# First MLP's input: seven block forms built behind one transposition of each token block

## The chip, the cores and the metric

The kernel runs on one core of one Trainium2 chip. The metric is device time in microseconds (us) of one execution. The core's engines run beside one another, each through a queue of its own: TensorE (PE in the profile; its weight loads are PEld), VectorE (DVE), ScalarE (ACT), GpSimd (POOL), and SyncE (SP), which here issues most of the transfers.

## The reference

A trunk of two layers over 1024 tokens of width 1024, all in float32. Layer 0 mixes tokens with a gated linear recurrence (HGRN2), layer 1 with a causal convolution module; a squared-ReLU MLP follows each mixer, with a layer norm after each part:

```python
for i in range(2):
    mix = hgrn2_mixer(x, ...) if i == 0 else conformer_conv_mixer(x, ...)
    x = layer_norm(ALPHA * x + mix, ln_mix_g[i], ln_mix_b[i])
    ff = jnp.square(jax.nn.relu(x @ ffn_w1[i])) @ ffn_w2[i]      # 1024 -> 4096 -> 1024
    x = layer_norm(ALPHA * x + ff, ln_ffn_g[i], ln_ffn_b[i])
```

The change is in layer 0, between the layer norm behind the mixer and `x @ ffn_w1[0]`.

## The kernel before, in words

**Split numbers.** A float32 operand is held as two parts, hi (a ScalarE copy that rounds) and lo (a VectorE subtraction of hi from the number), and a product is three TensorE passes, hi·hi, hi·lo and lo·hi. Making the two parts is called a split here (`split`, line 1042; for weights `Slots.split`, line 71).

**Block forms.** The first matrix product of the MLP is done as seven block products in place of eight. The input is four blocks: y[n] is the half n of the tokens (512 of them, as four token blocks t of 128), and k is the half of the 1024 columns; below, "nk" is the block of token half n and column half k. The seven products need the input in seven forms, all with the columns on the partitions, so transposed: form 1 is 00, form 2 is 01, form 5 is 00 − 10, form 6 is −(form 5) − 11, form 7 is 11 − 10, form 3 is 11, and form 4 is −(form 6) − 01. The weights come in seven forms as well, sums of four loaded blocks (`Forms.unit`, line 130). The product order is 1, 2, 6, 5, 7, 3, 4 for each of eight column groups c of the MLP; only at the start it is (c0, 1), (c0, 2), (c1, 1), (c1, 2), and then the others of c0 and of c1. One product of `Up.form` (line 1186 on) is twice 12 matmuls of 512 columns.

**Where the forms come from.** After the output projection of the mixer, `norm` (line 1091) finishes a token block y[n][:, t]. Before the change, forms 5, 6, 4 and 7 are made in token layout, by VectorE, 128x512 at a time (`forms_of`, line 1119, into the buffers `ts`, `t4s` and `t7s`), and each is then transposed by itself: `turn` (line 1096) does four 128x128 transpositions on TensorE into one of two PSUM banks (`aux`), and a split from that bank writes the form's slice for this t. In all there are seven such turns for each t, 28, so 112 transpositions.

**The order.** `bg.chores` is a list of closures, and each `product` takes one off the list behind its matmuls. From the end of the mixer on this is only the order of the program text: the framework's scheduler then lays the instructions of each engine, and of SP's queue, by text order among those whose inputs its own model holds ready. So the order in the trace can differ from that of the text. Waits follow whole buffers: a new view over the place of an old one waits until every access to the old one is done.

**Buffers that matter here** (in KB of each partition): `ts` at 200 and 202; the raw weight blocks of `Forms` at 192, 196, 200 and 204, so that the third lies over both `ts`; its sums at 160 and 162 on; its slots at 144, 152, 48, 112 and 120, where 144 holds the weights of (c1, 2) before and 48 is also the place of `t7s`; the layer norm's gain and offset at 192 and 196.

In the profile nearly all TensorE and VectorE work has line 204, the wrapper that counts costs. L1045 is the hi copy of a split, L72 that of the weights, L135 the load of a raw weight block, L1105 `keep` (the copy of y to HBM for the later residual), L1224 the first copy out of a product's bank.

Of the kernel before, what the change touches and what calls it, by code (L numbers as in the profile page):

```python
# [8 lines left out]
F32 = mybir.dt.float32  # L9
# [3 lines left out]
ALU = mybir.AluOpType  # L13
PSUM = bass.MemoryType.PSUM

P = 128
D = 1024
# [3 lines left out]
HT = 512  # L21
NTB = HT // P
# [141 lines left out]
class LateForms(Forms):  # L164

    turned = True
# [102 lines left out]
def body(ctx, tc, d, out):  # L269
    nc = tc.nc  # L270
# [9 lines left out]
    def view(kb, shape, dt=F32, name="t"):  # L280
        at, top = int(kb * 1024), KBYTES * 1024
        if at < edge[0]:
            if edge[0] < top:
                space.tile([P, (top - edge[0]) // 4], F32, name="gap")
            edge[0] = 0
        if at > edge[0]:
            space.tile([P, (at - edge[0]) // 4], F32, name="gap")
        edge[0] = at + (prod(shape) + 7) // 8 * 32
        return space.tile([P, *shape], dt, name=name)

    def ring(kbs, shape, name, dt=F32):
        return Ring([view(kb, shape, dt, name) for kb in kbs])

    def run(kb, n, size):
        return [kb + i * size for i in range(n)]

    def slots(kbs, name):
        return ring(kbs, (2, 1024), name, F32R)

    def raws(kbs, name="raw"):  # L300
        return ring(kbs, (1024,), name)
# [21 lines left out]
    bg = Background()  # L323
    vector = Clocked(nc.vector, bg.dve, vector_cost)
    tensor = Clocked(nc.tensor, bg.pe, tensor_cost)
# [6 lines left out]
    def aux():  # L332
        return rings["aux"]().rearrange("p (a b) -> p a b", a=NTB)
# [40 lines left out]
    ident = cst.tile([P, P], F32, name="ident")  # L374
    wide_t, rows = (HT,), (NTB, P)

    XF, VS, VO = {}, {}, {}
    x00, x10, x01, x11, t6 = [view(kb, (4, HT), F32, "xr") for kb in run(112, 5, 8)]
# [663 lines left out]
    def split(hi, lo, ps, scale=None):  # L1042

        if scale is None:
            nc.scalar.copy(out=hi, in_=ps)  # L1045
            vector.tensor_tensor(out=lo, in0=ps, in1=hi.bitcast(F32), op=ALU.subtract)
        else:
            nc.scalar.activation(hi, ps, AF.Copy, scale=scale)
            vector.scalar_tensor_tensor(out=lo, in0=ps, scalar=scale, in1=hi.bitcast(F32), op0=ALU.mult, op1=ALU.subtract)
# [7 lines left out]
    def gain(kb, name, layer):  # L1057
        return vec(kb, f"{name}_g", layer), vec(kb + 4, f"{name}_b", layer)
# [12 lines left out]
    def moments(yt):  # L1071
        bs = stat.tile([P, 2, 6], F32, tag="bs", name="bs")
        for j in range(2):
            half_stats(bs, yt, j)
        mv = rstd_of(bs)
        return mv[:, 0:1], mv[:, 3:4]
# [14 lines left out]
    def norm(yt, g, b):  # L1091
        mu, rs = moments(yt)
        vector.scalar_tensor_tensor(out=yt, in0=yt, scalar=mu, in1=g, op0=ALU.subtract, op1=ALU.mult)
        vector.scalar_tensor_tensor(out=yt, in0=yt, scalar=rs, in1=b, op0=ALU.mult, op1=ALU.add)

    def turn(yt, xt, t, k0, nk):

        for k in range(0, nk, 4):
            pt = aux()
            for j in range(4):  # L1100
                tensor.transpose(pt[:, j, :], yt[:, (k0 + k + j) * P : (k0 + k + j + 1) * P], ident)
            split(xt[:, 0, k : k + 4, t * P : (t + 1) * P], xt[:, 1, k : k + 4, t * P : (t + 1) * P], pt)

    def keep(half, t, src):
        nc.sync.dma_start(out=kept[half][t], in_=src)  # L1105
# [10 lines left out]
    def blocks(name, layer, c):  # L1116
        return [d[name][layer, c, q] for q in range(4)]

    def forms_of(x, out, only=(5, 6, 7, 4)):

        t = {i: out(i) for i in only}
        if 5 in only:
            vector.tensor_tensor(out=t[5], in0=x[0][0], in1=x[0][1], op=ALU.subtract)
            vector.scalar_tensor_tensor(out=t[6], in0=t[5], scalar=-1.0, in1=x[1][1], op0=ALU.mult, op1=ALU.subtract)
        if 7 in only:
            vector.tensor_tensor(out=t[7], in0=x[1][1], in1=x[0][1], op=ALU.subtract)
        if 4 in only:
            vector.scalar_tensor_tensor(out=t[4], in0=t[6], scalar=-1.0, in1=x[1][0], op0=ALU.mult, op1=ALU.subtract)
        return t
# [3 lines left out]


    g, b = gain(192, "ln_mix", 0)
    y = [view(160 + 16 * h, (NTB, D), F32, "y") for h in range(2)]
    for half in range(2):
        for t in range(NTB):
            nc.sync.dma_start(out=y[half][:, t], in_=d["x"][half * HT + t * P : half * HT + (t + 1) * P])
    ts, t4s = ring(run(200, 2, 2), wide_t, "t"), ring(run(212, 4, 2), wide_t, "t4")  # L1140
    early = [Slots(nc, vector, slots((204,), "fw"), raws((0,))), Slots(nc, vector, slots((112, 120), "fw"), raws((96, 100)))]
    early.append(Slots(nc, vector, slots((144,), "fw"), raws((152,))))

    xf = {i: view(kb, (2, 4, HT), F32R, f"x1f{i}") for i, kb in ((6, 0), (5, 16), (3, 32), (1, 64), (2, 80), (7, 96), (4, 128))}
    early[0].plan(blocks("w1q", 0, 0)[:1])
    early[1].plan([blocks("w1q", 0, 0)[1], blocks("w1q", 0, 1)[0]])
    early[2].plan(blocks("w1q", 0, 1)[1:2])
    yb = [[[y[n][:, t, k * HT : (k + 1) * HT] for n in range(2)] for k in range(2)] for t in range(NTB)]
    tt = {}

    def x1_form(t, i, src=None, k=0):
        turn(tt[t][i] if src is None else src, xf[i], t, k, 4)

    def x1_block(half, t):
        norm(y[half][:, t, :], g, b)
        if half == 0:
            bg.chores += [lambda: x1_form(t, 1, y[0][:, t, :]), lambda: x1_form(t, 2, y[0][:, t, :], 4)]
            return
        tt[t] = forms_of(yb[t], lambda i: (t4s if i == 4 else ts)(), (5, 6, 4))
        keep(0, t, y[0][:, t, :])  # L1160
        if t < NTB - 1:
            bg.chores += [lambda: x1_form(t, 6), lambda: x1_form(t, 5)]

    for half in range(2):
        for t, n in early_out + ((0, 1), (1, 1), (3, 0), (2, 1), (3, 1)) if half == 0 else [(t, n) for t in range(NTB) for n in range(2)]:
            ps = acc()
            if half or (t, n) not in early_out:
                product(ps, wide(oT[half], t, ws[n]))
            yv = y[half][:, t, n * HT : (n + 1) * HT]
            vector.scalar_tensor_tensor(out=yv, in0=yv, scalar=ALPHA, in1=ps, op0=ALU.mult, op1=ALU.add)  # L1170
            if n == 1:
                if half == 1 and t == 0:
                    early[0].ahead(1)
                x1_block(half, t)
                if half == 0 and t:
                    bg.chore()
# [232 lines left out]
            nc.sync.dma_start(out=raw, in_=d[name][at])  # L1409
            staged.append((name, at))  # L1410

    t7s = ring((48, 50), wide_t, "t7")
    fw = Forms(nc, vector, slots((144, 152, 48, 112, 120), "fw"), raws(run(192, 4, 4)), raws(run(160, 2, 4), "sum"), spare, 3, range(44))
    fw.todo = [[(blocks("w1q", 0, c), 2 if c < 2 else 0)] for c in range(NFC)]
    up = Up()

    def x1_late(t):
        turn(y[1][:, t, :], xf[3], t, 4, 4)
        tt[t].update(forms_of(yb[t], lambda i: t7s(), (7,)))
        x1_form(t, 7)  # L1420
        keep(1, t, y[1][:, t, :])

    late_forms = [lambda t=t: x1_late(t) for t in range(NTB)]
    bg.chores += [lambda: None] + late_forms[:1] + [lambda: x1_form(NTB - 1, 6), lambda: x1_form(NTB - 1, 5)] + late_forms[1:]
    bg.chores += [lambda t=t: x1_form(t, 4) for t in range(NTB)]
    up.form(0, 1, early[0].take(1)[0])
    up.form(0, 2, early[1].take(1)[0], late=True)
    up.form(1, 1, early[1].take(1)[0], ring((208, 210), wide_t, "c1"))
# [19 lines left out]
    y = [view(32 + 16 * h, (NTB, D), F32, "y") for h in range(2)]  # L1448
    fw = Slots(nc, vector, slots([112, 120, 144, 152, 128, 136, 168], "dw"), raws([192, 196, 200, 204, 160, 164], "dr"), spare, 6, range(10, 50))
    fh = Slots(nc, vector, slots([0, 8, 16, 24, 96, 104, 176], "dh"))  # L1450
    g, b = gain(184, "ln_ffn", 0)
# [61 lines left out]
    taken, turned, gate, normed = [0], [0], [None, [], None], [0]  # L1513
# [306 lines left out]
    y = [view(kb, (NTB, D), F32, "y") for kb in (88, 112)]  # L1820
    g, b = gain(184, "ln_ffn", 1)
# [102 lines left out]
```

## Time and profile before

| what | value |
|---|---|
| median of 3 runs | 2061.7 us (2056.03, 2061.7, 2062.01) |
| span of the profiled execution | 2068.3 us, 29719 instructions |
| TensorE busy | 2031.0 us, 98% |
| VectorE busy | 1482.9 us, 72% |
| ScalarE busy | 1090.2 us, 53% |
| GpSimd busy | 388.4 us, 19% |
| mean granted TensorE clock | 0.997 |

The span is the time from the first to the last instruction of one execution under the profiler; a time of that execution other than its span is not given. It is 6.6 us above the median of the runs. The runs themselves lie 6 us apart. Times on the trace are counted from the start of the span.

### The profile page before, as it was taken

To read this page: it belongs to the slowest core of one execution; us is meant where nothing else is said; L and a number is where in the kernel's file an instruction comes from. 1 tells how busy PE (TensorE), PEld (TensorE's weight loads), DVE (VectorE), ACT (ScalarE), POOL (GpSimd) and SP (SyncE) were. 2 spreads that over 40 slices of the span, in tenths; PEclk is the share of its full clock that TensorE was granted. 3 is DMA by queue.
4 is the path that set the end of the run, shared out by engine and by line. 5 is a ranking of instruction groups with operands and counts; after the bars stand their busy time and mean duration, and the time that the engine had idled before them with its cause. 6 is when DMAs were issued, how large, how long until landed. Compare 5 with 4: busy or idle time off the path is not lost. (4 is left out here: it accounts for less than half of the span.)

```text
span 2068.3 us, 29719 instructions
## 1 busy us (share of the span) xinstructions
PE 2031.0 (98%) x11192; PEld 1674.5 (81%) x11192; DVE 1482.9 (72%) x1976; ACT 1090.2 (53%) x1727; POOL 388.4 (19%) x387
## 2 busy tenths in 40 slices
PE   8999999999999999999999999999999999999998
PEld 7888777788888888888888888888878878888886
DVE  8698877877775666565567898889589666755556
ACT  5456555641464555444444776488625555343333
POOL 0112222111001000000001699079210000100002
PEclk9999999999999999999999999999999999999999
DMA  4778889852689786999998855587759778996542
GB/s 186 224 195 233 238 224 270 254 189 81 187 288 298 243 295 221 353 341 332 335 349 292 309 193 185 190 323 271 256 215 339 245 232 291 386 292 204 193 155 102
DMA packets 183944, 517.55 MB, mean 250 GB/s; under 512 B 17912, under 2 KB 49784, under 8 KB 182776
## 3 DMA queue, kind: packets, MB, share of 16 engines
q1 hardware_dynamic: 168312, 456.93, 62.6%
q0 software_dynamic: 15488, 58.72, 12.3%
q8 instruction: 87, 1.43, 0.3%
q14 instruction: 57, 0.47, 0.1%
HBM read 380.85 MB, written 201.85 MB: 282 GB/s over the span
## 5 line engine op out<-in xcount | busy, mean ns | idle before, releaser
L204 PE MATMUL ps<-dw,dh 128*128 128x512 f32 x2688 | 611.6, 389 | 1.9 <-ACT dh L72 1.1
L204 PEld LDWEIGHTS ps<-dw,dh 128*128 128x128 f32 x2688 | 504.1, 188 | 107.2 <-ACT dh L72 1.6
L204 PE MATMUL ps<-x1f,fw 128*128 128x512 f32 x1344 | 309.3, 390 | 2.3 <-DVE c L204 1.2
L204 PEld LDWEIGHTS ps<-x1f,fw 128*128 128x128 f32 x1344 | 251.1, 188 | 56.2 <-ACT c L1224 2.3
L204 PE MATMUL ps<-xf,fs 128*128 128x512 f32 x1008 | 249.3, 398 | 4.1 <-issue 1.9
L204 POOL TENSOR_TENSOR cb<-cb,prod 128x512 f32<-128x512 f32 x168 | 222.7, 1334 | 12.9 <-ACT prod L1555 2.3
L204 DVE TENSOR_TENSOR dh<-dh 128x1024 fp32r<-128x1024 f32 x112 | 136.4, 1222 | 117.3 <-ACT dh L72 117.1
L204 PEld LDWEIGHTS ps<-xf,fs 128*128 128x128 f32 x1008 | 184.5, 189 | 43.4 <-issue 2.1
L204 DVE SCALAR_TENSOR_TENSOR ps<-u,par,ps 128x512 f32<-128x512 f32 x296 | 206.2, 750 | 11.0 <-ACT ps L1567 9.5
L72 ACT CAST dh<-dh 128x1024 fp32r<-128x1024 f32 x112 | 117.4, 1051 | 163.7 <-DMA dh<-hf 163.7
L204 PE MATMUL ps<-xa,wa 128*128 128x512 f32 x864 | 203.1, 392 | 0.1
L204 PEld LDWEIGHTS ps<-xa,wa 128*128 128x128 f32 x864 | 160.3, 188 | 33.3 <-ACT ha L1289 0.3
L204 DVE TENSOR_TENSOR dw<-dr,dw 128x1024 fp32r<-128x1024 f32 x112 | 136.2, 1222 | 66.6 <-ACT dw L72 65.9
L72 ACT CAST dw<-dr 128x1024 fp32r<-128x1024 f32 x112 | 117.0, 1051 | 119.2 <-PE ps L204 100.2
L1555 ACT ACTIVATE prod<-u,par 128x512 f32<-128x512 f32 x168 | 119.8, 726 | 36.6 <-POOL cb L204 35.7
L518 POOL TENSOR_TENSOR mv<-mv,nhalf 128x1 f32<-128x1 f32 x32 | 43.3, 1355 | 407.6 <-DVE mv L204 407.6
L1408 POOL COPY next<-ss 128x1 f32<-128x1 f32 x38 | 21.2, 558 | 413.8 <-DVE spare L204 265.1
L204 PE MATMUL ps<-xb,wa 128*128 128x512 f32 x384 | 91.1, 393 | 0.0
L204 PE MATMUL ps<-w,oT 128*128 128x512 f32 x384 | 89.5, 391 | 1.3 <-ACT oT L932 0.8
L204 DVE TENSOR_TENSOR spare<-next,spare 128x1024 fp32r<-128x1024 f32 x38 | 46.5, 1224 | 60.6 <-ACT spare L1401 60.5
L204 PE MATMUL ps<-vw,xf 128*128 128x512 f32 x336 | 79.8, 399 | 6.0 <-ACT vw L435 5.2
L204 PEld LDWEIGHTS ps<-w,oT 128*128 128x128 f32 x384 | 71.5, 188 | 16.6 <-ACT oT L932 1.2
(236 smaller groups left out, 2959.6 us busy)
## 6 DMA issues: line engine op xcount, KB each, us to landing
wa<-ready SPq DMA_DIRECT2D x140, 512.0 KB, 5.5
dh<-hf SPq DMA_DIRECT2D x112, 512.0 KB, 5.3
sum_w<-in_w_dram POOLq DMA_DIRECT2D x40, 1024.0 KB, 10.9
ready<-spare SPq DMA_DIRECT2D x76, 512.0 KB, 4.6
raw<-in_w1q_dram SPq DMA_DIRECT2D x66, 512.0 KB, 4.4
dr<-sum_w SPq DMA_DIRECT2D x64, 512.0 KB, 5.7
hf<-ht SPq DMA_DIRECT2D x112, 256.0 KB, 4.9
dr<-in_w_dram SPq DMA_DIRECT2D x48, 512.0 KB, 5.3
```

What stands on the lines that cost most here:

```text
L72: self.nc.scalar.copy(out=slot[:, 0, c], in_=raw[:, c])
L204: return op(*args, **kw)
L518: nc.gpsimd.tensor_tensor(out=dst, in0=src, in1=nhalf[:, :n], op=ALU.pow)
L1408: nc.gpsimd.tensor_copy(out=raw[:, :1], in_=now)
L1555: nc.scalar.activation(tp, u[:, k : k + HT], AF.Copy, scale=tap(j, k))
```

## The change

Only the four blocks themselves are transposed now, each once. For the first token half nothing changes (forms 1 and 2). For the second, `x1_first(t)` turns block 10 and, on VectorE and from the PSUM bank, takes it from form 1, whose hi and lo are read back, which is form 5; `x1_second(t)` turns block 11 and makes form 6 from it. Both are split at once. The same step leaves forms 3, 7 and 4 unsplit in wide float32 buffers (`late_x`), and six chores `x1_late` split these in pieces of 128x1024. The two halves of y change places, `late_x[3]` and `late_x[7]` lie where y[0] was, `late_x[4]` where `t4s` was, `t7s` is gone, and `keep` stands right behind the norm for both halves.

```diff
-    y = [view(160 + 16 * h, (NTB, D), F32, "y") for h in range(2)]
+    y = [view(160 + 16 * h, (NTB, D), F32, "y") for h in range(2)][::-1]
-    ts, t4s = ring(run(200, 2, 2), wide_t, "t"), ring(run(212, 4, 2), wide_t, "t4")
+    ts = ring(run(200, 2, 2), wide_t, "t")
+    late_x = {4: view(212, (4, HT), F32, "x4")}
...
-    def x1_form(t, i, src=None, k=0):
-        turn(tt[t][i] if src is None else src, xf[i], t, k, 4)
+    def of(x, t, i=slice(None)):
+        return x[..., t * P : (t + 1) * P] if i == slice(None) else x[:, i, :, t * P : (t + 1) * P]
+
+    def turned(yt, k0):
+        pt = aux()
+        for j in range(4):
+            tensor.transpose(pt[:, j, :], yt[:, (k0 + j) * P : (k0 + j + 1) * P], ident)
+        return pt
+
+    def less(out, x, y):
+        vector.tensor_tensor(out=out, in0=x, in1=y, op=ALU.subtract)
+
+    def minus_both(out, x, y):
+        vector.scalar_tensor_tensor(out=out, in0=x, scalar=-1.0, in1=y, op0=ALU.mult, op1=ALU.subtract)
+
+    def x1_split(i, t, src):
+        split(of(xf[i], t, 0), of(xf[i], t, 1), src)
+
+    def x1_first(t):
+        s, pt = ts().rearrange("p (a b) -> p a b", a=4), turned(y[1][:, t, :], 0)
+        less(s, of(xf[1], t, 0).bitcast(F32), pt)
+        vector.tensor_tensor(out=s, in0=s, in1=of(xf[1], t, 1).bitcast(F32), op=ALU.add)
+        x1_split(5, t, s)
+        temp[t], x01[t] = s, pt
+
+    def x1_second(t):
+        s, pt = ts().rearrange("p (a b) -> p a b", a=4), turned(y[1][:, t, :], 4)
+        minus_both(s, temp[t], pt)
+        nc.scalar.copy(out=of(late_x[3], t), in_=pt)
+        less(of(late_x[7], t), of(late_x[3], t), x01[t])
+        x1_split(6, t, s)
+        x4 = of(late_x[4], t)
+        minus_both(x4, s, of(xf[2], t, 0).bitcast(F32))
+        less(x4, x4, of(xf[2], t, 1).bitcast(F32))
+
+    def x1_late(i, k):
+        split(xf[i][:, 0, k : k + 2], xf[i][:, 1, k : k + 2], late_x[i][:, k : k + 2])

     def x1_block(half, t):
         norm(y[half][:, t, :], g, b)
+        keep(half, t, y[half][:, t, :])
         if half == 0:
-            bg.chores += [lambda: x1_form(t, 1, y[0][:, t, :]), lambda: x1_form(t, 2, y[0][:, t, :], 4)]
+            bg.chores += [lambda k=k: turn(y[0][:, t, :], xf[1 + k // 4], t, k, 4) for k in (0, 4)]
             return
-        tt[t] = forms_of(yb[t], lambda i: (t4s if i == 4 else ts)(), (5, 6, 4))
-        keep(0, t, y[0][:, t, :])
+        if t == 0:
+            bg.done()
+            late_x.update({i: view(kb, (4, HT), F32, "xl") for i, kb in ((3, 176), (7, 184))})
         if t < NTB - 1:
-            bg.chores += [lambda: x1_form(t, 6), lambda: x1_form(t, 5)]
+            bg.chores += [lambda: x1_first(t), lambda: x1_second(t)]
...
-    t7s = ring((48, 50), wide_t, "t7")
...
-    def x1_late(t):
-        turn(y[1][:, t, :], xf[3], t, 4, 4)
-        tt[t].update(forms_of(yb[t], lambda i: t7s(), (7,)))
-        x1_form(t, 7)
-        keep(1, t, y[1][:, t, :])
-
-    late_forms = [lambda t=t: x1_late(t) for t in range(NTB)]
-    bg.chores += [lambda: None] + late_forms[:1] + [lambda: x1_form(NTB - 1, 6), lambda: x1_form(NTB - 1, 5)] + late_forms[1:]
-    bg.chores += [lambda t=t: x1_form(t, 4) for t in range(NTB)]
+    bg.chores += [lambda: None, lambda: x1_first(NTB - 1), lambda: x1_second(NTB - 1)]
+    bg.chores += [lambda i=i, k=k: x1_late(i, k) for i in (3, 7, 4) for k in (0, 2)]
```

## Rows read from the trace of the kernel before

**Rows 1.** The page: engines, busy us, share of span, instructions.

```profile
PE 2031.0 (98%) x11192; PEld 1674.5 (81%) x11192; DVE 1482.9 (72%) x1976; ACT 1090.2 (53%) x1727; POOL 388.4 (19%) x387
```

**Rows 2.** By stretch: length, busy PE, PEld, DVE, ACT, POOL, clock, DMA share, GB/s.

```profile
483.50:519.72 36.22, 36.22 (x175) 30.25 (x173) 26.93 (x41) 4.12 (x7) 4.35 (x3) 1.00 0.20 64
519.72:544.40 24.68, 24.68 (x123) 20.39 (x121) 18.57 (x26) 12.53 (x19) 1.45 (x1) 1.00 0.44 151
544.40:567.72 23.32, 22.33 (x115) 18.63 (x115) 16.02 (x21) 11.42 (x19) 2.13 (x2) 1.00 0.85 242
567.72:835.00 267.28, 265.94 (x1170) 218.72 (x1169) 175.73 (x209) 155.40 (x226) 10.64 (x17) 1.00 0.81 266
```

**Rows 3.** Waits of TensorE between 519 and 835: us, times, longest.

```profile
PE ps L204 <- DVE c L204: 1.2, 2, 1.0
PE ps L204 <- ACT c L1224: 1.1, 2, 0.7
```

**Rows 4.** Groups of transpositions on TensorE from 520.1 to 567.95: count, busy us, mean ns.

```profile
L204 PE MATMUL ps<-ident,t 128*128 128x128 f32 x40 | 6.2, 272 | 0.0
L204 PE MATMUL ps<-ident,y 128*128 128x128 f32 x16 | 2.4, 272 | 0.0
```

**Rows 5.** Timeline of TensorE: start us, us, operation, count, idle before and its releaser.

```profile
495.39 1.03 PE L204 MATMUL ps<-ident,t 128*128 128x128 f32 x8
...
545.43 3.91 PE L204 MATMUL ps<-x1f,fw 128*128 128x512 f32 x16 [0.99 <-DVE c L204]
549.19 0.60 PE L204 MATMUL ps<-ident,y 128*128 128x128 f32 x4
549.62 0.60 PE L204 MATMUL ps<-ident,t 128*128 128x128 f32 x4
549.98 6.16 PE L204 MATMUL ps<-x1f,fw 128*128 128x512 f32 x26
...
567.37 0.60 PE L204 MATMUL ps<-ident,t 128*128 128x128 f32 x4
567.72 98.83 PE L204 MATMUL ps<-x1f,fw 128*128 128x512 f32 x434
```

**Rows 6.** Splits by output, whole run: duration ns min/median/max, first and last start.

```profile
L204 DVE TENSOR_TENSOR x1f<-ps,x1f x28: 635/684/693, 464.4 to 573.2; 128x512 fp32r<-128x512 f32 x28
L1045 ACT CAST x1f<-ps x28: 578/587/612, 462.7 to 569.8; 128x512 fp32r<-128x512 f32 x28
L435 ACT CAST xf<-xr x28: 603/622/630, 3.7 to 59.1; 128x512 fp32r<-128x512 f32 x28
L435 ACT CAST xf<-s x2: 1042/1048/1053, 1556.4 to 1575.4; 128x1024 fp32r<-128x1024 f32 x2
L204 DVE TENSOR_TENSOR xf<-s,xf x2: 1225/1225/1225, 1557.4 to 1577.5; 128x1024 fp32r<-128x1024 f32 x2
```

**Rows 7.** VectorE's form operations in token layout, 483.4 to 575.

```profile
L204 DVE SCALAR_TENSOR_TENSOR t<-t,y 128x512 f32<-128x512 f32 x8 | 5.5, 683 | 0.0
L204 DVE TENSOR_TENSOR t<-y 128x512 f32<-128x512 f32 x8 | 5.4, 687 | 0.1
```

**Rows 8.** Timeline of SP's queue.

```profile
528.54 0.42 SPq L1105 DMA_DIRECT2D kept<-y  x1
536.30 6.47 SPq L135 DMA_DIRECT2D raw<-in_w1q_dram  x2
```

**Rows 9.** Timeline of VectorE: first sum of weights, and a bank's evacuation.

```profile
540.06 1.22 DVE L204 TENSOR_TENSOR sum<-raw 128x1024 f32<-128x1024 f32 x1 [2.44 <-DMA raw<-in_w1q_dram]
...
544.61 0.68 DVE L204 TENSOR_TENSOR c<-c,ps 128x512 f32<-128x512 f32 x1
```

**Rows 10.** Timeline of ScalarE: the hi copy of that sum.

```profile
541.32 1.06 ACT L72 CAST fw<-sum 128x1024 fp32r<-128x1024 f32 x1 [1.63 <-DVE sum L204]
```

**Rows 11.** Timeline of VectorE: end of the norm of t = 0 and of t = 3.

```profile
488.63 1.28 DVE L204 SCALAR_TENSOR_TENSOR y<-y,mv,ln_mix_b 128x1024 f32<-128x1024 f32 x1 [0.44 <-POOL mv L518]
...
526.85 1.29 DVE L204 SCALAR_TENSOR_TENSOR y<-y,mv,ln_mix_b 128x1024 f32<-128x1024 f32 x1 [0.44 <-POOL mv L518]
```

More of the change, by code (lines that the diff above doesn't have):

```diff
@@ L1147, in body @@
     early[2].plan(blocks("w1q", 0, 1)[1:2])
-    yb = [[[y[n][:, t, k * HT : (k + 1) * HT] for n in range(2)] for k in range(2)] for t in range(NTB)]
-    tt = {}
-    def x1_form(t, i, src=None, k=0):
-        turn(tt[t][i] if src is None else src, xf[i], t, k, 4)
+    temp, x01 = {}, {}
+    def of(x, t, i=slice(None)):
[5 more added lines that the diff above has]
+        return pt
```

## Prediction

> **What bounds the kernel now.** I read the page first: TensorE is busy 98% of the span, VectorE 72% [rows 1]. The kernel ends when TensorE is through, so an edit is worth what it takes out of TensorE's stream, plus or minus what TensorE stands waiting. Next, busy time by stretch. The change lies in three stretches: the output projection of the second token half (483.50 to 519.72), the first four products of the MLP (to 544.40), and the products of column group 0 in which the last forms arrive (to 567.72). TensorE is busy through the first two without a break, loses 0.99 us in the third, and the granted clock is 1.00, the 2.4 GHz level, in all of them; the rest of this MLP loses 1.3 us of 267 [rows 2]. Then TensorE's waits: from 519 to 835 they are 2.3 us in all [rows 3]. So almost nothing can be gained here by better waiting, and all that counts is instructions removed from TensorE. Last, the timelines, for the price of one such instruction and for what stands close behind TensorE.
>
> Dense 512-column matmuls start every 0.228 us (98.83 us for 434 [rows 5]); a product of 24 is 5.5 us.
>
> **What leaves TensorE.** Before, 28 turns of four transpositions; now 16, four for each block and t. The first half's eight are the same. Between 483.5 and 520 the turns were two for each of t = 0 to 2 (forms 6 and 5) and still are two (blocks 10 and 11). So the twelve turns, 48 transpositions, all leave the time after 519.72: there were 56 there [rows 4], and there will be 8. The price is read from start to start. Eight in a row, 549.19 to the next matmul at 549.98, take 0.79 us; four in a row, 567.37 to 567.72, take 0.35 us [rows 5]. In the trace the 56 stand in four places with eight (from 526.17, 541.36, 549.19 and 555.97) and six with four (535.00, 535.67, 558.45, 561.44, 565.54, 567.37): 4 x 0.79 + 6 x 0.35 = 5.26 us. What stays is one place with eight: 5.26 − 0.79 = 4.47 us leave, 1.49 of them before 544.4 and 2.98 after. Bounds: twelve turns at 0.35 are 4.2, at 0.44 (the first four of eight, 549.19 to 549.62) 5.3.
>
> Each transposition's own duration is 272 ns [rows 4], near three times its spacing, since they overlap. The Trainium skill, "TensorE: Matmul & The Clock Gate", Part 4: PE-mode transpose, gives about 275 ns for one in a kernel and says that the clock's full rate does not engage for them. The duration agrees with the trace; by the page's figure an estimate of the change's worth would be 48 x 0.275 = 13.2 us. The clock does not: it reads 1.00 through stretches with 56 of them [rows 2, 4], so I give nothing for a clock that fewer transpositions might free.
>
> **What VectorE and ScalarE do instead.** Before, per t: four form operations in token layout (8 and 8 in all, 0.69 and 0.68 us [rows 7]) and five split subtractions from the bank (0.68 [rows 6]): 36 of 128x512, 24.6 us. Now per t eight of 128x512 (two for form 5, one each for 6 and 7, two for 4, and two splits), 32, for which I take the same 0.68, 21.8 us, whether an operand lies in a bank or not (those of rows 6 and 7 differ by 0.01); and six wide subtractions at 1.225, the price of the same step in layer 1 [rows 6], 7.4 us. Together 29.2, so 4.6 us more. ScalarE: twenty copies from the bank at 0.587 are 11.7 us; now four of those, eight from SBUF at 0.622 and six wide at 1.048 [rows 6] are 13.6, so 1.9 us more. Neither is on TensorE's path as long as there is room: VectorE is busy 61.5 of the 84.2 us of the three stretches [rows 2], and would be 66.1 of 79.7. But it moves: in the first stretch fifteen such operations (two of them just behind its end) become 24, and 26.9 us of 36.2 become 33, or 91%; after it, 21 become eight and six wide, 1.5 us less. ScalarE has 28 of 84 us. I price all this at nothing; if the cover goes, what TensorE feels is a late norm or a late form, taken up in the rivals.
>
> **What moves.** `keep` of the second half is written earlier in the text, but the last of the eight already goes out at 528.54, right behind the last norm (ended 528.14) [rows 8, 11]; nothing moves in SP's queue, and nothing is gained or lost. The smaller buffers that go (`t4s`, `t7s`) free slot 48 for weights earlier, which nobody on TensorE waited for [rows 3]: nothing.
>
> **The one wait that can change.** TensorE has the first four products done at 519.72 + 96 x 0.228 + 0.79 = 542.4 now, instead of 544.4, and needs weights that come through a chain. The third raw block lies over both `ts` buffers. Before, the transpositions at 535.67 were the last readers; the load went out at 536.30 [rows 8], the first sum began at 540.06 when it landed [rows 9], its hi copy ended at 542.38 [rows 10]. TensorE then still stood until 545.43, for a bank whose evacuation at 544.61 was queued behind other VectorE work [rows 5, 9]. Now `ts` is last read by form 6's split and by form 4's first step for t = 3. From the norm's end at 528.14 [rows 11]: both turns 0.8, six VectorE operations up to that step 4.1, the step 0.7, two evacuations in between 1.4, one ScalarE copy that cannot hide 0.6: 535.7, about when they came free before. So the load, and the weights at 542.4, come when they came, and TensorE arrives with them. Behind its loads SP holds little else there [rows 8]. I take the wait as unchanged, 0.99 us. Its lower bound is 0 (the copy is done as TensorE arrives); its upper bound is that the six wide splits, 6 x 1.225 = 7.4 us, get in front of form 4's step: the wait is then about 7.4.
>
> **Sum.** −4.5 from TensorE, 0 from the wait, 0 from the rest: 2061.7 − 4.5 = 2057.2. The profiled span, 2068.3, would become 2063.8; it lies 0.32% over the median of the runs, and I carry over the difference only. Bounds: −5.3 − 1.0 = −6.3 (2055.4) to −4.2 + 6.4 = +2.2 (2063.9). A measurement of this kernel can tell about 0.3%, 6.2 us, from no change: most of my forecast lies inside that.
>
> **Rivals.**
> *Weights late.* The wait before column group 0 grows by half of its bound up to all of it, 3.7 to 7.4 us in place of 0.99: −4.5 + 2.7 to 6.4, middle 0.0, 2061.7. For it: text order puts the splits of forms 3 and 7 near the first sums, and TensorE arrives 2 us sooner. Against: the load lands when VectorE has stood idle for 2.44 us [rows 9], room for two wide splits.
> *VectorE falls behind in the first stretch* (the slower one). At 91% the norm of a block queues behind the eight operations of the block before it. If the scheduler still puts a block's turns one product behind, TensorE's queue stops at them. Price: half of the eight operations, 2.7 us, on three blocks, and on t = 3, whose norm ended at 528.14, 2.9 us after the place that the text gives its first turn (518.93 + 0.8 + 5.5 = 525.2): 8.1 + 2.9 = 11.0 us, so 2061.7 − 4.5 + 11.0 = 2068.2. It decides from 1.1 us for each of the four. Against: t = 0's turns stood at 495.39, 5.5 us behind their norm's end at 489.91, with no idle time [rows 5, 11].
> *The small waits go too.* Buffers come free earlier (`t7s`, y), and the 2.3 us of rows 3 vanish: 2061.7 − 4.5 − 2.3 = 2054.9. Against: rows 3's second wait is behind a ScalarE copy that the change does not touch.
> *Each transposition holds TensorE for its whole 272 ns* [rows 4]: 48 x 0.272 = 13.1, 2048.6. Against it, eight fit in 0.79 us [rows 5]. This is what the page named above would make of it.
>
> **How the numbers follow.** Forecast (2055.4 to 2060) 0.52; weights late 0.20; small waits go 0.13; VectorE behind 0.11; whole durations 0.04. The likeliest gives 2057.2. For 8 in 10: the forecast, small waits and the most part of the late weights, so 2052.5 (below 2054.9 by what the runs scatter) to 2064. Faster by over 0.3% is below 2055.5: two thirds of the small waits, the whole durations, and a third of the forecast, because the median before is near the top of its runs: 0.30. Slower by over 0.3% is above 2067.9: most of VectorE behind, and a bit for a later stretch that the scheduler lays worse: 0.11. Within it 0.59.
>
> **What would show it.** Right: 16 turns in all, eight transpositions after 519.7; forms' first products beginning at the same place, and the matmul that stood at 567.72 some 4.5 us earlier; TensorE gapless from 483 to 520; a wait of about 1 us ahead of column group 0; wide splits of about 1.05 and 1.22 us done before their products. Wrong: TensorE waits on `y` or on a bank between 490 and 530 (VectorE behind), on the weights' sum or copy at 542 (weights late), or waits anywhere behind 570, where the scheduler has all instructions to lay anew.

## The result, and the profile after

The changed kernel takes 2068.43 us (median of 5 runs, 2067.28 to 2073.75) against 2061.7 (5 runs): ratio 1.0041, 95% interval 1.0026 to 1.0055, so 5.4 to 11.3 us slower. The forecast was 2057.2 us and its range ended at 2064.0.

The two profiled spans differ by 2.0 us only, because the execution of before spends 7.7 us more ahead of the output projection, where both do the same. So the traces are compared stage by stage, each from its own start. The output projection takes 97.8 us before and 97.5 after. The first MLP's first product (first matmul with `x1f` to the first with `dh`, "the stage" from here on) takes 315.1 us before (519.7 to 834.8) and 323.1 after (511.7 to 834.8). Behind the stage, where both do the same, after takes 2.0 us more (1235.5 against 1233.5); run 2 below, all but the same kernel, takes 1232.9, and all kernels lie between 1228.6 and 1235.5 there, with small waits of TensorE's at changing places. So the 8.0 us of the stage are what the traces show of the change's loss.

The page of the changed kernel, engines (answers to [rows 1]):

```profile
PE 2029.2 (98%) x11144; PEld 1670.9 (81%) x11144; DVE 1489.2 (72%) x1978; ACT 1093.1 (53%) x1725; POOL 386.2 (19%) x387
```

48 instructions fewer on TensorE, as drawn up; VectorE has 6.3 us more, ScalarE 2.9 more. By stretch, with the columns of [rows 2]:

```profile
475.44:511.66 36.22, 36.22 (x175) 30.16 (x173) 28.32 (x44) 5.59 (x9) 4.36 (x3) 1.00 0.18 61
511.66:539.60 27.94, 23.45 (x111) 19.12 (x110) 24.93 (x34) 18.15 (x26) 1.45 (x1) 0.99 0.49 158
539.60:550.00 10.40, 8.03 (x19) 5.40 (x20) 9.87 (x9) 3.07 (x4) 1.26 (x1) 0.54 1.04 283
550.00:834.80 284.80, 281.55 (x1231) 231.67 (x1230) 178.56 (x211) 159.34 (x231) 10.78 (x18) 0.99 0.78 256
```

The first stretch is as full as before. In the second TensorE is busy 23.45 of 27.94 us, and in the third it does 19 matmuls in 10.4 us, at a mean granted clock of 0.54. TensorE's waits from 505 to 840 (answers to [rows 3], 2.3 us in all there):

```profile
PE ps L204 <- ACT fw L72: 6.7, 2, 4.5
PE ps L204 <- DVE c L204: 1.8, 1, 1.8
PE ps L204 <- ACT c L1261: 1.4, 2, 0.9
PE ps L204 <- DVE fw L204: 0.2, 1, 0.2
```

10.1 us, and 6.9 of them are for the weights of column group 0 (`fw`). The timeline of TensorE (answers to [rows 5]):

```profile
513.36 0.60 PE L204 MATMUL ps<-ident,y 128*128 128x128 f32 x4
513.72 12.32 PE L204 MATMUL ps<-x1f,fw 128*128 128x512 f32 x53
525.87 0.60 PE L204 MATMUL ps<-ident,y 128*128 128x128 f32 x4
...
526.54 0.60 PE L204 MATMUL ps<-ident,y 128*128 128x128 f32 x4
526.89 8.21 PE L204 MATMUL ps<-x1f,fw 128*128 128x512 f32 x35
539.60 2.07 PE L204 MATMUL ps<-x1f,fw 128*128 128x512 f32 x4 [4.49 <-ACT fw L72]
543.84 2.07 PE L204 MATMUL ps<-x1f,fw 128*128 128x512 f32 x4 [2.17 <-ACT fw L72]
546.12 116.89 PE L204 MATMUL ps<-x1f,fw 128*128 128x512 f32 x508 [0.20 <-DVE fw L204]
...
716.11 118.87 PE L204 MATMUL ps<-x1f,fw 128*128 128x512 f32 x516 [1.83 <-DVE c L204]
```

The last row's place before:

```profile
717.46 117.52 PE L204 MATMUL ps<-x1f,fw 128*128 128x512 f32 x516 [0.22 <-DVE c L204]
```

Twelve transpositions are left in the stage (one turn of t = 2 slid behind its first matmuls), not eight. Then the chain that the waits stand for. SP's queue (answers to [rows 8]):

```profile
518.79 13.34 SPq L135 DMA_DIRECT2D raw<-in_w1q_dram  x2
```

The second of the two issues is the third raw block: it goes out near the row's end, at 531.80, 20.1 us into the stage; before, 16.6 (536.30 − 519.72). VectorE, from the norm of t = 3 on (answers to [rows 9, 11]):

```profile
516.20 1.28 DVE L204 SCALAR_TENSOR_TENSOR y<-y,mv,ln_mix_b 128x1024 f32<-128x1024 f32 x1
...
521.11 0.68 DVE L204 TENSOR_TENSOR xl<-xl,ps 128x512 f32<-128x512 f32 x1
...
527.18 0.69 DVE L204 TENSOR_TENSOR t<-x1f,ps 128x512 f32<-128x512 f32 x1 [2.24 <-PE ps L204]
...
531.09 0.69 DVE L204 TENSOR_TENSOR x1f<-t,x1f 128x512 fp32r<-128x512 f32 x1
...
534.02 2.35 DVE L204 TENSOR_TENSOR x1f<-xl,x1f 128x1024 fp32r<-128x1024 f32 x2
536.30 1.22 DVE L204 TENSOR_TENSOR sum<-raw 128x1024 f32<-128x1024 f32 x1
...
538.03 2.35 DVE L204 TENSOR_TENSOR x1f<-xl,x1f 128x1024 fp32r<-128x1024 f32 x2
540.30 1.22 DVE L204 TENSOR_TENSOR x1f<-x,x1f 128x1024 fp32r<-128x1024 f32 x1
541.44 1.22 DVE L204 TENSOR_TENSOR sum<-sum,raw 128x1024 f32<-128x1024 f32 x1
...
544.84 2.35 DVE L204 TENSOR_TENSOR fw<-sum,fw 128x1024 fp32r<-128x1024 f32 x2
```

The norm ends at 517.48, but its block's first turn stands 8.4 us further on in TensorE's queue. The two banks of `aux` take turns, and the one that this turn writes was last read by t = 2's form 7 (`xl<-xl,ps`), until 521.79: so 4.3 of the 8.4 us are given by the program, and the other 4.1 by the order that the scheduler chose. The last reader of the `ts` buffers ends at 531.78, and the load goes out with it. Two wide splits then stand before the first sum, three between it and the second, and a sixth (543.71) before the lo parts. ScalarE (answers to [rows 10]):

```profile
531.77 3.89 ACT L1045 CAST x1f<-xl 128x1024 fp32r<-128x1024 f32 x4
...
538.52 1.03 ACT L72 CAST fw<-sum 128x1024 fp32r<-128x1024 f32 x1
...
542.74 1.04 ACT L72 CAST fw<-sum 128x1024 fp32r<-128x1024 f32 x1 [2.66 <-DVE sum L204]
```

The first hi copy comes 1.0 us behind its sum (ended 537.52); the second waits for a sum that VectorE does behind three wide splits. Last, the clock (length, five engines, granted clock, DMA share, GB/s):

```profile
535.00:540.00 5.00, 0.51 (x2) 0.40 (x2) 5.00 (x6) 5.00 (x7) 0.00 (x0) 0.90 0.61 201
540.00:542.00 2.00, 1.67 (x4) 0.76 (x3) 2.00 (x3) 0.08 (x1) 0.00 (x0) 0.50 1.04 352
...
546.00:548.00 2.00, 1.89 (x5) 1.50 (x6) 2.00 (x3) 0.00 (x0) 0.00 (x0) 0.50 1.01 203
548.00:550.00 2.00, 2.00 (x8) 1.58 (x7) 1.47 (x2) 0.50 (x1) 0.00 (x0) 0.69 1.06 274
```

Behind the wait of 4.49 us the clock is at 0.50, the 1.2 GHz level, for some 9 us; from 550 on it is 1.00.

### The profile page after: what moved, and what is told of

Its sections match the earlier page's. It is cut to its first block, busy times and chain, and to the rows that moved or that the text cites. A ratio compares the mean times of both kernels' runs of the same rounds, so it can differ in the third digit from the quotient of the medians.

```text
span 2070.3 us, 29615 instructions
## 1 busy us (share of the span) xinstructions
PE 2029.2 (98%) x11144; PEld 1670.9 (81%) x11144; DVE 1489.2 (72%) x1978; ACT 1093.1 (53%) x1725; POOL 386.2 (19%) x387
## 4 chain that ended last, share of the span: by engine, by line
PE 65%; DMA 17%; DVE 8%; issue 5%; ACT 3%; POOL 2%; SPq 0%; DVEq 0%; POOLq 0%; ACTq 0%
PE ps L204 65%; DMA sum_w<-in_w_dram 7%; DMA next<-in_wpw_dram 2%; POOL cb L204 1%; DMA dh<-hf 1%; DMA next<-in_w1q_dram 1%; DMA y<-kept 1%; DMA sum_w<-sum_w 1%; DMA hf<-hr 1%; DMA vr<-in_wv_dram 1%; ACT spare L1438 1%; DVE xf L204 1%; DVE qk L204 1%; DVE ps L204 1%; DMA raw<-in_w1q_dram 0%
## 5 line engine op out<-in xcount | busy, mean ns | idle before, releaser
L204 PE MATMUL ps<-x1f,fw 128*128 128x512 f32 x1344 | 312.6, 394 | 10.1 <-ACT fw L72 6.7
L204 PEld LDWEIGHTS ps<-w,oT 128*128 128x128 f32 x384 | 71.4, 188 | 16.6 <-ACT oT L932 1.2
```

What stands on the lines that cost most here:

```text
L204: return op(*args, **kw)
```

## Experiments

Theory: `ts` comes free late, so the third raw block and the weights are late, and the wide splits stand in front of what is left of their chain. Rivals: the splits alone; VectorE's load as such; transpositions that cost more or less than their spacing. All kernels were timed in five rounds beside the kernel before. Where nothing else is said, the diff is against the changed kernel.

| kernel | median us | ratio, 95% interval | stage us | waits in it us |
|---|---|---|---|---|
| before (medians beside the others) | 2058.57 to 2061.7 | | 315.1 | 2.3 |
| after | 2068.43 | 1.0041 (1.0026 to 1.0055) | 323.1 | 10.1 |
| 1 own buffers | 2056.04 | 0.9985 (0.9971 to 0.9998) | 312.1 | 4.5 |
| 2 splits later in the text | 2069.08 | 1.0038 (1.0022 to 1.0053) | 322.7 | 9.4 |
| 3 both | 2057.78 | 0.9984 (0.9970 to 0.9998) | 311.5 | 2.9 |
| 4 splits held | 2059.43 | 1.0002 (0.9991 to 1.0013) | 314.1 | 5.2 |
| 5 narrow pieces | 2058.95 | 0.9999 (0.9986 to 1.0011) | 313.5 | 4.5 |
| 6 before, load held | 2062.14 | 1.0020 (1.0010 to 1.0031) | 313.5 | 1.4 |
| 7 before, more turns | 2065.48 | 1.0022 (1.0010 to 1.0034) | 313.5 | 1.3 |
| 8 the wait filled | 2066.57 | 1.0039 (1.0027 to 1.0052) | 322.8 | 6.0 |
| 9 job at the 36th | 2057.50 | 0.9994 (0.9982 to 1.0006) | 312.0 | 4.2 |
| 10 job at 33 | 2051.31 | 0.9965 (0.9952 to 0.9978) | 309.9 | 2.7 |
| 11 job at 31 | 2058.04 | 0.9991 (0.9979 to 1.0002) | 314.4 | 4.9 |
| 12 own buffers again | 2056.45 | 0.9992 (0.9978 to 1.0006) | 311.3 | 4.2 |

Runs 6 and 7 leave the stage's matmuls and its waits nearly as they were, and have 313.5 both, 1.6 us less than the one traced execution of before, some 1 us of it in waits: so a difference below 2 us between two stages, each traced once, tells nothing.

**1. Own buffers for the fourth tile's temporaries.** Two 2 KB buffers at 48 and 50, so that `ts` is last used for t = 2.

```diff
-        s, pt = ts().rearrange("p (a b) -> p a b", a=4), turned(y[1][:, t, :], 0)
+        s, pt = (last_ts[0] if t == NTB - 1 else ts)().rearrange("p (a b) -> p a b", a=4), turned(y[1][:, t, :], 0)
...
+    last_ts.append(ring((48, 50), wide_t, "t3"))
```

> The changed kernel with one edit: the two temporaries of t = 3 lie where the t7 buffers were (48 and 50 KB), so that the third raw weight block no longer waits for them. Theory 1 (the load behind the temporaries is what makes TensorE stand at column group 0): the load goes out some 10 us sooner, the first sum no longer waits for it, the 4.5 and 2.2 us waits in front of column group 0 fall under 1.5 us, the clock stays at 1.00, and the first MLP product stage, 323.1 us in the changed kernel and 315.1 before, becomes 309 to 312; total 2055 to 2059, ratio to before 0.996 to 0.999. Theory 2 (VectorE and ScalarE are simply full between 530 and 548 with the wide splits): the load comes sooner but sum and copies still stand behind the splits, the waits shrink by less than half, and the stage stays at 317 to 322.

Measured: 11 us less in the stage than after. The loads, VectorE and TensorE of this kernel:

```profile
519.38 16.31 SPq L135 DMA_DIRECT2D raw<-in_w1q_dram  x4
```

```profile
527.77 0.69 DVE L204 TENSOR_TENSOR t<-x1f,ps 128x512 f32<-128x512 f32 x1 [2.24 <-PE ps L204]
528.37 1.22 DVE L204 TENSOR_TENSOR sum<-raw 128x1024 f32<-128x1024 f32 x1
```

```profile
536.68 117.21 PE L204 MATMUL ps<-x1f,fw 128*128 128x512 f32 x516 [0.98 <-DVE c L204]
...
707.20 117.27 PE L204 MATMUL ps<-x1f,fw 128*128 128x512 f32 x516 [2.03 <-DVE c L204]
```

The third raw block goes out at 523.89, 11.6 us into the stage (after: 20.1), the first sum starts 16.1 us in (after: 24.6), and TensorE is back at 0.98 us of wait, for the same releaser as before. The theory holds. The turns and all the splits are those of the changed kernel, so VectorE's load as such is not the cause.

**2. The wide splits five chores later, form 7 first.**

```diff
-    bg.chores += [lambda i=i, k=k: x1_late(i, k) for i in (3, 7, 4) for k in (0, 2)]
+    bg.chores += [lambda: None] * 5 + [lambda i=i, k=k: x1_late(i, k) for i in (7, 3, 4) for k in (0, 2)]
```

> The changed kernel with one edit: the six wide splits stand five chores later in the text, behind the first four products, in the order 7, 3, 4. Theory 1: the third raw block still lands when it did, about 1 us after TensorE has arrived; the copy and the lo part of the first sum then follow at once, so TensorE waits 3 to 5 us in place of 9 (4.5 + 2.2 + the lo parts), and the stage becomes 314 to 318 us. Theory 2: with the wide splits out of the way the weights are made in time and the stage becomes 309 to 312.

A miss: waits of 4.50 and 2.16 us at the same places, stage 322.7. VectorE's and ScalarE's rows around these waits follow one another as after: the text's order moved nothing, presumably because these splits are ready long before in the scheduler's model. So it tells nothing of the splits, and serves as a repeat of the changed kernel.

**3. Both.** The edits of 1 and 2 together.

> Both edits: own place for the temporaries of t = 3 and the wide splits behind the first four products. Theory 1: as the first of them alone, stage 309 to 312, total 2055 to 2059. Theory 2: as the second alone or better, 309 to 312. If either theory leaves out a third cause (the clock, transfers, the later stages laid anew), it stays above 313.

Stage 311.5, as in 1 within what executions differ by; the text order again adds nothing.

**4. The wide splits held by data.** Each takes one column, through a one-column copy, from the lo part of the first two weight forms (the column is overwritten by the split itself); the chores also stand later in the text, much as in run 2, and the buffers are those of the changed kernel.

```diff
+        nc.vector.tensor_copy(out=xf[i][:, 0, k, :1], in_=made_first[k // 2][:, 1, :1].bitcast(F32))
         split(xf[i][:, 0, k : k + 2], xf[i][:, 1, k : k + 2], late_x[i][:, k : k + 2])
...
+            if (c, i) == (0, 6):
+                made_first += [f, fw.queue[0]]
```

> The changed kernel, buffers as they are (the third raw block still waits for the temporaries of t = 3), but each wide split is held by a one-column copy from the lo part of the first two weight forms of column group 0, so that it can't stand in front of them in VectorE's or ScalarE's queue. Theory 1 (the late load is the cause, the splits only lengthen it): the first sum starts at the same place, about 1 us after TensorE has arrived; its copy and lo part follow at once; TensorE waits some 4 to 5 us in place of 9, the stage goes from 323 to 315 to 318 us. Theory 2 (the splits in the queues are the cause, the load is harmless): the wait falls to about 1 us and the stage to 309 to 312.

The load goes out as late as after (20.1 us into the stage), yet the stage is 314.1, between what the two theories said. TensorE:

```profile
540.51 1.20 PE L204 MATMUL ps<-x1f,fw 128*128 128x512 f32 x4 [2.79 <-ACT fw L72]
542.31 18.01 PE L204 MATMUL ps<-x1f,fw 128*128 128x512 f32 x71 [0.59 <-ACT fw L72]
```

From the start of the stage until column group 0 runs on without a stop it is 24.4 us in run 1, 28.0 here and 34.5 after (546.12). But here four matmuls of that group are done by then, and after eight, 0.9 us for each four. Without them, the late load is worth about 2.7 us, and the splits in front, given the late load, about 5.5 with the lower clock among them. The other 2.8 of the 11.0 us between run 1 and after come later, nearly all by the lower clock. Either cure alone takes most of it, since the splits find room when the load is early, and the load does little when they are not there.

**5. Twelve narrow pieces in place of six wide ones**, on kernel 3.

```diff
-        split(xf[i][:, 0, k : k + 2], xf[i][:, 1, k : k + 2], late_x[i][:, k : k + 2])
+        for t in (k, k + 1):
+            x1_split(i, t, of(late_x[i], t))
```

> The kernel with both edits (own buffers, splits later in the text), but the last three forms are split in twelve pieces of 128x512 in place of six of 128x1024. VectorE has 12 x 0.69 = 8.2 us in place of 7.4, ScalarE 12 x 0.62 = 7.4 in place of 6.3. As nothing that TensorE waits for stands behind them there, I expect no difference from the wide pieces: stage 311 to 313, total within 2 us of it. If width matters, the stage is 314 or more.

No difference was expected, and the stage is 2.0 us longer: narrow pieces get in front in the queues (waits of 0.69, 2.85 and 0.69 us around column group 0, where kernel 3 has 0.98). Two executions differ by nearly as much, so this is no more than a hint in favour of wide pieces.

**6. The kernel before, its third raw load held** behind t = 3's split of form 5, to price a late load alone.

```diff
+            if len(a) == 3 and self.behind:
+                self.nc.vector.tensor_copy(out=a[-1][:, :1], in_=self.behind.pop())
...
+    fw.behind = [xf[5][:, 1, 0, HT - 1 :].bitcast(F32)]
```

> The kernel before with one edit: the third raw block of column group 0 is loaded only when the split of form 5 for t = 3 is done, by a one-column copy into it, some 1.7 to 2.2 us later than it went out (536.3 in the trace of before). Nothing else of the change is in it. Theory 1: TensorE's wait of 0.99 us in front of column group 0 grows by about that much, to 2.5 to 3.5 us; stage 316 to 318.5 in place of 315.1. If the load has slack, as a theory that blames the splits alone needs, the wait stays near 1 us and the stage near 315.

A miss in size: the load went out 1.4 us later, the waits became 0.95 and 0.48 us, now for the weights, and the stage (313.5) shows no loss. Before, the load had some room, because TensorE waited for a bank that came later than the weights' hi copy [rows 5, 10]. The median is 2 to 6 us above before's; its one profile doesn't show where, and that stays open.

**7. The kernel before with 48 more transpositions** in the first half's turns, in the output projection.

```diff
-            for j in range(4):
+            for j in list(range(4)) * (1 + (extra.pop() if extra else 0)):
```

> The kernel before, with 48 transpositions more: the eight turns of the first token half do each of their transpositions twice or three times into the same bank, nothing else changed. If one costs its spacing (0.079 to 0.11 us), it is 4 to 5.5 us slower than before, ratio 1.002 to 1.0027. If one costs its whole duration of 0.272 us, 13 us, ratio 1.0063. If TensorE had room there, nothing.

The output projection takes 103.1 us in place of 97.8: 5.3 us, 0.11 for each, and the ratio says 2.1 to 7.0. The rows of the 24 in one place:

```profile
453.30 2.78 PE L204 MATMUL ps<-ident,y 128*128 128x128 f32 x24
```

Spacing, not the 272 ns of one, is the price.

**8. The wait filled.** 44 transpositions of the identity behind the fourth product, not used by anything.

```diff
+    pt = aux()
+    for j in range(44):
+        tensor.transpose(pt[:, j % 4, :], ident, ident)
```

> The changed kernel with 44 more transpositions of the identity tile (128 columns each, result not used) put into TensorE's queue between the fourth product and column group 0, where it waited 4.49 us in the changed kernel; the weights' load, the wide splits and the buffers stay as they are. In the changed kernel the granted clock fell to 0.50 in the 8 us behind that wait, and the stage took 323.1 us. 44 at the spacing of 0.1 to 0.11 us that the 48 additional ones had are 4.4 to 4.8 us, so they take the place of the wait. Theory 'the wait lowers the clock, and that costs 4 to 5 us on top': the clock stays near 1.00 behind it, the stage falls to 318 to 320 us and the total by 3 to 5 us against the changed kernel, though TensorE does more. Rival 'the clock falls for another reason, or its loss is hidden': the stage stays at 323 us or more. If the clock falls all the same behind the second wait (2.17 us), the stage lies between, near 321.

A miss in size. TensorE and the clock:

```profile
537.10 4.96 PE L204 MATMUL ps<-ident 128*128 128x128 f32 x44
541.82 1.18 PE L204 MATMUL ps<-x1f,fw 128*128 128x512 f32 x4
545.99 2.07 PE L204 MATMUL ps<-x1f,fw 128*128 128x512 f32 x4 [2.99 <-ACT fw L72]
```

```profile
542.00:544.00 2.00, 1.00 (x5) 0.47 (x3) 2.00 (x3) 0.25 (x1) 0.00 (x0) 1.00 1.04 367
544.00:546.00 2.00, 0.01 (x1) 0.01 (x1) 2.00 (x3) 1.07 (x2) 1.26 (x1) 0.76 1.00 385
546.00:548.00 2.00, 2.00 (x4) 1.15 (x4) 2.00 (x2) 1.02 (x1) 0.00 (x0) 0.50 0.94 215
```

Where the filling stood, the clock stayed at 1.00 and the four matmuls took 1.18 us in place of 2.07. Behind the second wait, now 2.99 us, it fell all the same. So the fall does follow the wait. But filling the first wait gained nothing, and the stage, 322.8, is unchanged: the second group of four starts 32.2 us into the stage in both kernels, when its weights are copied, and the 0.9 us that the first group won came back as 0.8 of longer wait (2.99 in place of 2.17). What the clock costs behind the second wait this run did not take away.

**9 to 11. The second wait.** In kernels 1, 3 and after, TensorE waits 1.8 to 2.0 us for an addition of VectorE's (`c<-c,ps`), 191 to 203 us into the stage; before waited 0.22 at that matmul. There ScalarE's queue stands at the copy of one background load-and-split job (`spare`), and VectorE's behind it. ScalarE and VectorE in run 1, then in run 10:

```profile
704.24 1.05 ACT L1439 CAST spare<-next 128x1024 fp32r<-128x1024 f32 x1 [3.46 <-DMA next<-in_wpw_dram]
...
699.43 0.68 DVE L204 TENSOR_TENSOR c<-c,ps 128x512 f32<-128x512 f32 x1
705.32 1.22 DVE L204 TENSOR_TENSOR spare<-next,spare 128x1024 fp32r<-128x1024 f32 x1 [5.21 <-ACT spare L1439]
706.46 0.68 DVE L204 TENSOR_TENSOR c<-c,ps 128x512 f32<-128x512 f32 x1
```

```profile
704.90 1.05 ACT L1439 CAST spare<-next 128x1024 fp32r<-128x1024 f32 x1 [2.21 <-issue]
...
699.74 1.28 DVE L204 TENSOR_TENSOR c<-c,ps 128x512 f32<-128x512 f32 x2
...
705.99 1.23 DVE L204 TENSOR_TENSOR spare<-next,spare 128x1024 fp32r<-128x1024 f32 x1 [2.03 <-ACT spare L1439]
```

Run 9 lists on kernel 3 the job places by hand, with the 35th form's job at the 36th; runs 10 and 11 on kernel 1, with the job at 32 put at 33 and at 31; the other places are those of the rule that the list replaces. The edit of run 10:

```diff
-    fw = Forms(nc, vector, slots((144, 152, 48, 112, 120), "fw"), raws(run(192, 4, 4)), raws(run(160, 2, 4), "sum"), spare, 3, range(44))
+    fw = Forms(nc, vector, slots((144, 152, 48, 112, 120), "fw"), raws(run(192, 4, 4)), raws(run(160, 2, 4), "sum"), spare, 8, (3, 6, 8, 11, 14, 16, 19, 22, 24, 27, 30, 33, 35, 38, 40, 43))
```

> The kernel with both edits, and one background job (the copy of a later stage's weights, run when a weight form is made) moved from the 35th form to the 36th. In the traces with own buffers TensorE waits 1.9 to 2.0 us some 193 us into the stage (0.2 us in the kernel before), because VectorE's and ScalarE's queues stand behind that job's transfer. If that is where part of the saving went, the wait goes, the stage is 309 to 310.5 us (311.5 without the edit) and the total 1 to 2 us lower. If the wait only moves to another job, nothing is won.

> The changed kernel with own buffers for the fourth tile's temporaries (stage 312.1 us, wait of 2.03 us for VectorE about 195 us into the stage), and the one load-and-split job that is issued at product group 32 issued at 33 instead (the others at the same places, now listed by hand). Theory 'ScalarE stands behind the copy of that job, whose transfer is late, and VectorE's addition of a finished column group behind that': the wait moves or goes; if it goes, the stage is about 310 us and the total 1 to 2 us below the kernel with own buffers alone. Rival 'any place collides with some addition': a wait of 1 to 2 us stays at another place and the total stays at 2056 to 2057 us.

> As the run with the job at 33, but issued at 31, one product group earlier than in the kernel with own buffers. By the same theory the transfer lands before ScalarE comes to the copy: the wait of 2.03 us goes, the stage is about 310 us and the total 1 to 2 us below the kernel with own buffers alone. Rival 'any place collides': 2056 to 2057 us.

Run 9 is a miss: the wait stays, 1.95 us; it moved another job. Run 10: the wait is gone, the stage is 309.9 us and the kernel 0.22 to 0.48% faster than before, the best of the study. The transfer is no earlier: from its issue to the copy it is 4.7 us in both runs (699.58 to 704.24 in run 1, 700.16 to 704.90 in run 10). What changed is the order on VectorE: two of its additions (`c<-c,ps`) now stand ahead of the job's step, where run 1 has one, and the one for which TensorE waited (706.46) is among them. Run 11: TensorE waits 1.27 us near that place for a ScalarE copy (`c`) queued behind the job's, so the collision moved to another engine. Its longest wait, 2.65 us, comes 139 us in, ahead of the moved job, behind a transfer (`hf<-ht`) for which VectorE stood idle 5.97 us (3.55 in run 1), and is not shown to be the job's; the stage is 314.4. So the theory's queue behind the job holds, what cures it is the order and not an earlier transfer, and at 31 the rival holds.

**12. Kernel 1 again**, on the chip of runs 8, 10 and 11.

> The changed kernel with own buffers for the fourth tile's temporaries once more, on the chip of the three runs beside it, so that they can be compared with it: 0.997 to 1.000 of the kernel before, stage 312 us, and the 2.0 us wait about 195 us into it.

Stage 311.3, the wait 1.71 us. Run 10's stage is 1.4 us below it, and its median 5.1 us; but the trace is of this kernel's fastest execution (2053.32 of a median 2056.45) and of the second slowest of run 10 (2053.67 of 2051.31), and the profiled spans are alike (2051.5 and 2051.9). So the larger part of those 5.1 us was not found in any stage.

## Why the prediction was wrong

*48 transpositions leave, 4.5 us*: right in count and price. With twelve left in the stage it is 5.26 − 3 x 0.35 = 4.2 us there. The stage without its waits is 312.1 to 312.8 us in the kernel before and runs 6 and 7, and 307.1 to 308.6 in runs 1, 3, 9, 10 and 12: the saving is there, whenever the weights are in time. *The rival of whole durations* fell with run 7.

*VectorE's and ScalarE's more work at nothing*: right in the first stretch, where TensorE has no gap and VectorE 28.3 us, not 33; *VectorE falls behind* did not happen, and that its 2068.2 meets the measured 2068.43 is luck. *The small waits go too* did not come either: behind the start of column group 0 they are 3.3 us after (0.53, 0.89 and 1.83) in place of 1.3. Pricing the added work at nothing was wrong in the second stretch, where the step below took the cover away.

*The one wait that can change* is the step that failed. It put the release of `ts` at 535.7, 16.0 us into the stage, by a chain from the end of t = 3's norm: both turns at once, then VectorE. The turns stood 8.4 us behind that norm in TensorE's queue, and the release came 20.1 us in, though the norm itself ended 2.6 us earlier in the stage than before. Before, VectorE worked first and the turn was the last reader; now the turn comes first and seven VectorE operations behind it. The chain left out both the bank that t = 2 still held and the place in the queue; what kept the scheduler from an earlier turn once the bank was free was not tried and stays open. The step's upper bound had the second half of the cause, the wide splits in front (worth about 5.5 us by run 4), and the rival *Weights late* named the right mechanism and the right size of wait: 3.7 to 7.4 us, and 6.9 came. What spoke against it, VectorE idle for 2.44 us before the load landed, was true of before only.

That rival's price was too low for two terms that no step had. The clock: the two groups of four matmuls took 2.07 us where they take 1.20 at full rate (run 4), 1.7 together (0.9 of which would else have been waited, by run 8), and the next 508 took 116.89 us where 0.2277 for each (98.83 for 434 [rows 5]) makes 115.7, 1.2. And the wait at 716.11, 1.83 us in place of 0.22, with 118.87 us for the 516 matmuls behind it against 117.52 before, 1.35. The sum for the stage: −4.2 for the turns, +7.8 for waits (10.1 − 2.3), +4.3 for the clock, +7.9; measured +8.0.

## To carry to other kernels

When a step that ended with TensorE is turned round so that it ends with VectorE, look at what lies over its buffers: the next load waits for the last reader, and two separate buffers of 2 KB decided here between 0.4% slower and 0.1% faster (0.02 to 0.29% in run 1; run 12's interval takes in no change). Reckon such a release from where the queue puts the instruction and not from when its input is ready, and count work with a later deadline that becomes ready at that moment as standing in front; it is held by data, not by text order. Add to a wait of TensorE's of several us the matmuls behind it at the lower clock, unless another wait behind them swallows what they lose.

## What the runs showed of the hardware

The clock falls behind short waits too, and not always. Behind waits of 1.83 us (after), 1.76 (run 2), 1.90 (run 8) and 1.93 (run 3), the next 516 matmuls took 118.85 to 118.89 us; behind 2.03 (run 1), 1.95 (run 9) and 1.71 (run 12) 117.25 to 117.27. So the same kind of wait costs 1.6 us more in some of these kernels' executions. Runs 3 and 9, each from about 1 us behind the end of its wait (706.83 and 704.96); the clock is the third number from the end:

```profile
708.00:710.00 2.00, 2.00 (x7) 1.50 (x6) 1.77 (x3) 1.53 (x4) 0.00 (x0) 0.50 0.17 68
```

```profile
706.00:708.00 2.00, 2.00 (x10) 1.68 (x9) 1.77 (x4) 1.54 (x4) 0.00 (x0) 1.00 0.22 88
```

The Trainium skill, "TensorE: Matmul & The Clock Gate", Part 1: The HAM clock gate (the "warmup" mystery), gives 1.2 GHz as the rate after TensorE has idled. The trace agrees: 0.50 behind 4.49 us; behind 1.9 us it was 0.50 in run 3 and 1.00 in run 9. The same section says that the number of slow matmuls at a kernel's start varies between runs of one kernel; no run here shows that, and the one kernel traced twice (runs 1 and 12) kept 1.00 behind both waits.
